# The S5 group's state carried over every fourth token instead of every second

## The chip, the cores and the metric

The kernel runs on one core of a Trainium2 chip. The metric is the device time of one execution in microseconds (us); before the change it was 1253.27 us (median of three runs, 1252.76 to 1253.33).

Names used below: TensorE (PE in the profile; its weight loads are PEld), VectorE (DVE), ScalarE (ACT), GpSimd (POOL) and SyncE (SP, which issues nearly all DMAs). SBUF is the on-chip memory, PSUM the accumulators that TensorE writes.

## The reference

One layer of a streaming encoder over 16 learned meta tokens and 256 tokens (T = 272 in all), D_MODEL = 2048, everything in float32: RMSNorm, one projection, two groups of heads side by side (HGRN2, a gated recurrence, and S5, a diagonal complex state-space model), one output projection, and a gated MLP with a short convolution. The part that the change rewrites is the S5 group: 64 channel groups of 16 inputs and 64 complex states each.

```python
def s5_mixer(u, lam_re, lam_im, log_step, b_re, b_im, c_re, c_im, d_skip, w_glu, b_glu, gain):
    ...
    ab_re = mag * jnp.cos(a_im * dt)
    ab_im = mag * jnp.sin(a_im * dt)
    ...
    bb_re = z_re[..., None] * br - z_im[..., None] * bi
    bb_im = z_re[..., None] * bi + z_im[..., None] * br
    bu_re = jnp.einsum('blgh,gph->lbgp', ug, bb_re)
    bu_im = jnp.einsum('blgh,gph->lbgp', ug, bb_im)
    ...
    _, _, st_re, st_im = lax.associative_scan(_complex_scan_combine, (a_seq_re, a_seq_im, bu_re, bu_im), axis=0)
    y = (jnp.einsum('lbgp,ghp->blgh', st_re, c_re.astype(f32))
         - jnp.einsum('lbgp,ghp->blgh', st_im, c_im.astype(f32)))
    y = y.reshape(b_sz, seq_len, D_S5) + d_skip.astype(f32) * uf
    y = jax.nn.gelu(y)
    y = y * jax.nn.sigmoid(y @ w_glu.astype(f32) + b_glu.astype(f32))
    return rmsnorm(y, gain)
```

## The kernel before

**The large products.** The projection `w_in` is worked off in chunks of 256 output columns, in the order `u0 h0 u1 h1 u2 h2 u3 h3 g0 g1 g2 g3` (u: S5 inputs, h: the HGRN2 heads' parts, g: their output gates). Each weight of 1 MB comes by one DMA on SP's queue (`raw`), ScalarE casts it to a rounded half `whi` (L160) and VectorE takes the rest, `wlo = raw - whi` (helper `tt`, L82); three buffers of each. `mm3` then multiplies three ways: high by high, high by low, low by high (L184 to L186, output `acc`, 272 columns). One `wlo` tile serves 24 of these matmuls. The MLP's gate and up products (`ga`, `ua`) and the down product (`d`) follow much later and are not touched.

**The S5 group** is worked in eight blocks j of 128 channels (8 channel groups, four pairs q of two groups). The 272 tokens are split into even and odd ones (TH = 136 of each), and the state is carried over every second token only. For a block:

- `s5_b(j)` prepares its tables: POOL multiplies B by the step (`bt1`, `bt2`, `br`), ScalarE copies `cp` from `cpc` (the output matrices, as they are and multiplied by the step) and lays out `eb`, TensorE transposes it (`btp`), and makes `ktp`, the direct product of C and B, from which ScalarE makes the short-range kernel `k0`.
- `s5_u`, `s5_split` copy the block's inputs into `ysb` and scatter them by four DMAs into `R`.
- `s5_tile(j)`: TensorE projects (`bu`, two rows of the array at a time, 64 rows by 128 columns). For each pair, `s5_scan` builds a table of rotations `W` of 136 columns from the 17 columns of `ew` by three doublings on ScalarE and VectorE, with the powers `pw[6]`, `pw[7]`, `pw[8]` (17, 34 and 68 steps), rotates `bu` (`P<-W,bu`), POOL adds the two halves (`m`), VectorE scans real and imaginary part (two scans of 136) and rotates back (`P<-W,m`, `xo`). TensorE then adds the short-range kernel (`yps<-ysb,k`, one matmul of 136 columns) and the states through `cp` (`yps<-xo,cp`), for even and odd tokens.
- Behind that stand GELU, the GLU product on the 258 columns from token T0 = 14 on, and the norm.

**The set-up** in front of it: POOL builds the powers `pw` of the rotation one from the other (`cpow`, per level two products `pt`, their sum `pw` and a negation) and, interleaved, the table `ew` of 16 columns by four doublings through `scb`; VectorE copies the 17th column (`ew<-pw`, L472) and makes `cpc`.

**The order.** The Tile framework schedules all instructions against a model of time and gives each engine one list, which it works off strictly in order; an instruction that waits holds back all behind it on its engine. Priorities (`pri`) tilt that order; the three-way products are given a lower priority than the rest and fill what is left.

Two places set how the S5 group meets the other work:

```python
        with pri(wpri[0]):
            pe.matmul(accs[m], lh, xh[:, n0:n1], start=first, stop=False)
```

```python
    for o in ORDER.split():
        {"u": do_u, "h": do_h, "g": do_g}[o[0]](int(o[1]))
```

The head work that shows up in the lists beside it is HGRN2's: `q`, `PP`, `SP`, `qh`, `kt`, `lps`, `dps`, `vtp`, `S`.

## Time and profile before

| | before |
|---|---|
| median of three runs | 1253.27 us |
| the profiled execution: its own time | 1252.36 us |
| its span | 1250.6 us |
| mean granted TensorE clock | 0.994 |
| TensorE busy | 1226.9 us |
| VectorE busy | 873.7 us |
| ScalarE busy | 601.2 us |
| POOL busy | 117.0 us |
| bytes read from HBM | 206.12 MB |

The profile is of one execution. A row of a view names the line of the kernel, the engine, the operation, the tile that is written and what is read, and shapes as partitions x elements. Lines of helpers stand for all that use them (L82 is every `tensor_tensor`, L91 every `scalar_tensor_tensor`, L79 every activation), so there the tile names tell the work. An idle time in front of an instruction is put down to the semaphore that came last. Matmul ends are modelled: what a matmul costs in the stream is read from the starts. A float32 matmul leaves two records.

### The profile page before, as it was taken

To read this page: it belongs to the slowest core of one execution; us is meant where nothing else is said; L and a number is where in the kernel's file an instruction comes from. 1 tells how busy PE (TensorE), PEld (TensorE's weight loads), DVE (VectorE), ACT (ScalarE), POOL (GpSimd) and SP (SyncE) were. 2 spreads that over 40 slices of the span, in tenths; PEclk is the share of its full clock that TensorE was granted. 3 is DMA by queue.
4 is the path that set the end of the run, shared out by engine and by line. 5 is a ranking of instruction groups with operands and counts; after the bars stand their busy time and mean duration, and the time that the engine had idled before them with its cause. 6 is when DMAs were issued, how large, how long until landed. Compare 5 with 4: busy or idle time off the path is not lost.

```text
span 1250.6 us, 22795 instructions
## 1 busy us (share of the span) xinstructions
PE 1226.9 (98%) x9299; PEld 1151.9 (92%) x9299; DVE 873.7 (70%) x1516; ACT 601.2 (48%) x1042; POOL 117.0 (9%) x165
## 2 busy tenths in 40 slices
PE   7989999999999999999999999999999999999997
PEld 6979898989989999999999999999999988888886
DVE  8989999999748867765665656656656645554554
ACT  5646767574545446343433433433434434444454
POOL 5483132221000000000000000000000000000000
PEclk9989999999999999999999999999999999999999
DMA  8533344243444565565556555555555545555552
GB/s 256 147 122 113 105 144 136 86 134 127 144 135 136 169 201 172 167 203 179 192 172 199 171 196 173 193 178 187 184 181 191 210 166 198 202 188 187 197 205 98
DMA packets 176298, 210.82 MB, mean 169 GB/s; under 512 B 14773, under 2 KB 168880, under 8 KB 170416
## 3 DMA queue, kind: packets, MB, share of 16 engines
q1 hardware_dynamic: 175871, 209.26, 51.1%
q8 instruction: 73, 1.20, 0.4%
q14 instruction: 34, 0.27, 0.1%
q0 software_dynamic: 320, 0.09, 0.0%
HBM read 206.12 MB, written 2.10 MB: 166 GB/s over the span
## 4 chain that ended last, share of the span: by engine, by line
PE 92%; DVE 3%; POOL 2%; issue 1%; DMA 1%; ACT 0%; SPq 0%; DVEq 0%; ACTq 0%; POOLq 0%
PE acc L186 9%; PE acc L184 8%; PE acc L185 8%; PE ua L185 7%; PE ua L184 7%; PE ga L184 7%; PE ua L186 7%; PE ga L186 7%; PE ga L185 7%; PE d L970 6%; PE d L969 6%; PE d L968 6%; PE lps L713 1%; PE bu L600 1%; DVE xn L91 1%
## 5 line engine op out<-in xcount | busy, mean ns | idle before, releaser
L82 DVE TENSOR_TENSOR wlo<-raw,whi 128x1024 fp32r<-128x1024 f32 (+1 forms) x376 | 461.4, 1227 | 320.8 <-ACT whi L160 271.2
L160 ACT CAST whi<-raw 128x1024 fp32r<-128x1024 f32 (+1 forms) x382 | 397.8, 1042 | 519.9 <-PE ga L185 158.3
L184 PE MATMUL ga<-fh,whi 128*128 128x258 f32 x704 | 199.0, 283 | 0.5 <-DVE a L82 0.5
L186 PE MATMUL ga<-fh,wlo 128*128 128x258 f32 x704 | 198.5, 282 | 0.0
L185 PE MATMUL ua<-fl,whi 128*128 128x256 f32 x704 | 198.4, 282 | 0.0
L185 PE MATMUL ga<-fl,whi 128*128 128x258 f32 x704 | 198.1, 281 | 0.0
L186 PE MATMUL ua<-fh,wlo 128*128 128x256 f32 x704 | 197.9, 281 | 0.0
L184 PE MATMUL ua<-fh,whi 128*128 128x256 f32 x704 | 197.9, 281 | 0.0
L186 PE MATMUL acc<-xh,wlo 128*128 128x272 f32 (+1 forms) x640 | 186.7, 294 | 5.0 <-DVE wlo L82 5.0
L185 PE MATMUL acc<-xl,whi 128*128 128x272 f32 (+1 forms) x640 | 186.1, 292 | 3.9 <-DVE xl L82 3.9
L184 PE MATMUL acc<-xh,whi 128*128 128x272 f32 (+1 forms) x640 | 186.4, 294 | 0.4 <-ACT PP L79 0.4
L184 PEld LDWEIGHTS ga<-fh,whi 128*128 128x128 f32 x704 | 133.0, 189 | 0.7 <-DVE a L82 0.7
L185 PEld LDWEIGHTS ga<-fl,whi 128*128 128x128 f32 x704 | 133.5, 190 | 0.0
L184 PEld LDWEIGHTS ua<-fh,whi 128*128 128x128 f32 x704 | 133.1, 189 | 0.0
L186 PEld LDWEIGHTS ua<-fh,wlo 128*128 128x128 f32 x704 | 132.9, 189 | 0.0
L185 PEld LDWEIGHTS ua<-fl,whi 128*128 128x128 f32 x704 | 132.8, 189 | 0.0
L186 PEld LDWEIGHTS ga<-fh,wlo 128*128 128x128 f32 x704 | 132.6, 189 | 0.0
L186 PEld LDWEIGHTS acc<-xh,wlo 128*128 128x128 f32 x640 | 121.4, 190 | 9.4 <-DVE wlo L82 5.6
L185 PEld LDWEIGHTS acc<-xl,whi 128*128 128x128 f32 x640 | 121.6, 190 | 7.5 <-DVE xl L82 4.8
L968 PE MATMUL d<-whi,ah 128*128 128x512 f32 x328 | 127.7, 389 | 0.0
L969 PE MATMUL d<-whi,al 128*128 128x512 f32 x328 | 127.6, 389 | 0.0
L184 PEld LDWEIGHTS acc<-xh,whi 128*128 128x128 f32 x640 | 121.1, 190 | 4.1 <-issue 2.0
(381 smaller groups left out, 1868.1 us busy)
## 6 DMA issues: line engine op xcount, KB each, us to landing
raw<-in_w_ffn_gate SPq DMA_DIRECT2D x44, 1024.0 KB, 5.1
raw<-in_w_ffn_up SPq DMA_DIRECT2D x44, 1024.0 KB, 5.1
raw<-in_w_ffn_down SPq DMA_DIRECT2D x44, 1024.0 KB, 4.8
raw<-in_w_in SPq DMA_DIRECT2D x39, 1024.0 KB, 5.2
raw<-in_w_out SPq DMA_DIRECT2D x16, 1024.0 KB, 5.8
raw<-in_w_glu SPq DMA_DIRECT2D x4, 1024.0 KB, 5.2
x<-in_x SPq DMA_DIRECT2D x4, 512.0 KB, 5.7
out<-ob SPq DMA_DIRECT2D x8, 256.0 KB, 2.7
```

What stands on the lines that cost most here:

```text
L82: eng.tensor_tensor(out=dst, in0=a, in1=b, op=op)
L91: dve.scalar_tensor_tensor(out=dst, in0=a, scalar=s, in1=b, op0=op0, op1=op1, **kw)
L160: act.copy(out=hi[:, c], in_=raw[:, hf, c])
L184: pe.matmul(accs[m], lh, xh[:, n0:n1], start=first, stop=False)
L185: pe.matmul(accs[m], lh, xl[:, n0:n1], start=False, stop=False)
L186: pe.matmul(accs[m], ll, xh[:, n0:n1], start=False, stop=end)
L600: return pe.matmul(bus[i][:, ri], bt[h, 2 * ri + q0 // 2], R[h, q0 // 2], start=True, stop=True)
L713: pe.matmul(ps[:, i], lhs[i], qf[:, 64 * i:64 * (i + 1)], start=True, stop=True)
L968: pe.matmul(dps[t][n], ah[:, tk], hi, start=False, stop=False, skip_group_check=True)
L969: pe.matmul(dps[t][n], al[:, tk], hi, start=False, stop=False, skip_group_check=True)
L970: pe.matmul(dps[t][n], ah[:, tk], lo, start=False, stop=end, skip_group_check=True)
```

## The change

The state is carried over every fourth token. TH becomes 68, tokens are held in four phases, and the tables and instructions are regrouped:

- Four channel pairs share an instruction: `s5_rot` builds one `W` of four times 68 columns by two doublings (`pw[7]`, `pw[8]`: 17 and 34 steps), the products `P`, `m` and `xo` are 4 x 68 wide, and one scan of 544 elements takes the place of eight of 136 per block. Its factor is a table `r4t` that is zero at each pair's first column. `m` is added on VectorE, no longer on POOL. Buffers of `bu`, `W`, `P`, `m`, `xo`, `bt` and the kernels go to one each.
- `bu` is projected by matmuls of 64 rows by 64 columns and 68 tokens (128 of them for 64 of twice the width and twice the columns).
- The short range reaches over three tokens: three kernels `kz`, from `ktp` (48 columns for 32) by a masked product `kw` on VectorE and three transposes `kwp`, streaming 204, 136 and 68 columns. `yps<-xo` is 32 matmuls of 68 or 67 columns per block for 16 of 136 or 135.
- `cpc` and `cp` have four kinds rather than two; POOL computes the two new ones from the old by `a2`, the step of two tokens, in eight instructions. B is multiplied by one and by two steps on POOL.
- `R` is scattered by eight DMAs per block instead of four; the powers are 1 to 64, 68 and 136 (not 34), so the 17th column of `ew` takes `pw[6]`, and the doublings of `ew` start one level later.
- The S5 columns behind are 260 (four phases of 65) for 258; `w_out` reads 258 of them, from QS = 2 on.

Lines move by four: L82 is now L86, L88 L92, L91 L95, L160 L164, L184 to L186 L188 to L190.

```diff
+NPH = 4
-TH = T // 2
-K0 = T0 // 2
+TH = T // NPH
+K0 = T0 // NPH
...
-    NPW = [1, 2, 4, 8, 16, 32, 34, 68, 136]
+    NPW = [1, 2, 4, 8, 16, 32, 64, 68, 136]
...
-    for d_, a_, b_ in ((1, 0, 0), (2, 1, 1), (3, 2, 2), (4, 3, 3), (5, 4, 4), (6, 5, 1), (7, 6, 6), (8, 7, 7)):
+    for d_, a_, b_ in ((1, 0, 0), (2, 1, 1), (3, 2, 2), (4, 3, 3), (5, 4, 4), (6, 5, 5), (7, 6, 2), (8, 7, 7)):
         cpow(d_, a_, b_)
+    a2 = s5p.tile([128, 2, NP], F32, name="a2")
+    tt(a2, pw[:, 1, 1:3], r2.unsqueeze(1).to_broadcast([128, 2, NP]), MUL, pool)
...
-    for lv, n in ((1, 1), (2, 2), (3, 4), (4, 8)):
+    for lv, n in ((2, 1), (3, 2), (4, 4), (5, 8)):
...
-        dve.tensor_copy(out=ew[:, :, k, 16:17], in_=pw[:, 5, k].unsqueeze(2))
+        dve.tensor_copy(out=ew[:, :, k, 16:17], in_=pw[:, 6, k].unsqueeze(2))
...
+    for hb in range(2):
+        cv = cpc[:, 16 * hb:16 * hb + 16]
+        c4 = [z.rearrange("p j h -> p (j h)").rearrange("p (j k r h) -> p j k r h", k=2, r=2, h=S5H)
+              for z in (cth[0], cth[1])]
+        for z, w in zip(c4, (a2[:, 0], a2[:, 1])):
+            tt(z.rearrange("p j k r h -> p j (k r h)"), cv[:, :, 0:2].rearrange("p j k r h -> p j (k r h)"),
+               w[:, 16 * hb:16 * hb + 16].unsqueeze(2).to_broadcast([128, 16, 4 * S5H]), MUL, pool)
+        tt(cv[:, :, 2:4, 0], c4[0][:, :, :, 0], c4[1][:, :, :, 1], ADD, pool)
+        tt(cv[:, :, 2:4, 1], c4[0][:, :, :, 1], c4[1][:, :, :, 0], SUB, pool)
...
+        for n, ar, ai in ((1, abr[:, js], xi[:, js]), (2, a2[:, 0, js], a2[:, 1, js])):
+            src, dst = bp[:, 4 - n:4], bp[:, 4 - 2 * n:4 - n]
...
+            for t, a in ((t1, ar), (t2, ai)):
+                tt(t[:, 0:n].rearrange("p s r j h -> p (s r) j h"), src.rearrange("p s r j h -> p (s r) j h"),
+                   a.unsqueeze(1).unsqueeze(3).to_broadcast([128, 2 * n, 4, S5H]), MUL, pool)
...
+        ktp = ptp.tile([128, 3, S5H], F32, tag="tp", name="ktp")
         for ri in range(2):
             for q in range(4):
+                pe.matmul(ktp[32 * q:32 * q + 32], cp[:, q, 0, ri].rearrange("p g h -> p (g h)"),
+                          bp[:, 1:4, ri, q], start=(ri == 0), stop=(ri == 1), skip_group_check=True)
...
+        tt(kw, ktp.unsqueeze(2).to_broadcast([128, 3, 8, S5H]),
+           misc[:, 26:34].unsqueeze(1).unsqueeze(3).to_broadcast([128, 3, 8, S5H]), MUL)
+        tp = ptp.tile([128, 3, 128], F32, tag="tp", name="kwp")
+        for k in range(3):
+            pe.transpose(tp[:, k], kw[:, k].rearrange("p g h -> p (g h)"), ident)
+        act.copy(out=kz, in_=tp)
...
+            for g in range(2):
+                c = 32 * q + 16 * g
+                sp.dma_start(out=R[h:h + 64, q % 2, g], in_=ysb[c:c + 16, j])
...
+        for lv, n in ((7, 17), (8, 34)):
+            c, sn = (pw[:, lv, i, js].unsqueeze(1).unsqueeze(3).to_broadcast([128, 2, 4, n]) for i in (1, 2))
+            tmp, tmq = (P[:, i].rearrange("p b (j n) -> p b j n", j=4) for i in range(2))
+            tt(tmp[:, :, :, 0:n], W[:, 0:2, :, 0:n], sn, MUL)
+            tt(tmq[:, :, :, 0:n], W[:, 1:3, :, 0:n], c, MUL)
+            tt(W[:, 1:3, :, n:2 * n], tmq[:, :, :, 0:n], tmp[:, :, :, 0:n], ADD)
+            fact(W[:, 0, :, n:2 * n], W[:, 2, :, n:2 * n], AF.Copy, scale=-1.0)
...
+                    for g in range(2):
+                        gr = slice(64 * g, 64 * g + 64)
+                        pe.matmul(bu[gr, i, (2 * ri + p) * TH:(2 * ri + p + 1) * TH], bt[h, 2 * ri + p, gr], R[h, p, g],
+                                  start=True, stop=True)
...
+        dve.tensor_tensor_scan(out=mf, data0=r4t[0].rearrange("p r j k -> p (r j k)"),
+                               data1=mf, initial=0.0, op0=MUL, op1=ADD)
+        tt(P, rot(None), m.unsqueeze(1).to_broadcast([128, 2, 2, 4 * TH]), MUL)
...
+        for k in range(3):
+            pe.matmul(yps[:, k:3], kz[:, 2 - k], ysb[:, j, 0:3 - k], start=(k == 0), stop=False, skip_group_check=True)
+        for p in (3, 0, 1, 2):
+            o, c, n0 = (0, 0, 0) if p == 3 else (1, p + 1, 1)
+            for ri in range(2):
+                for q in range(4):
+                    pe.matmul(yps[32 * q:32 * q + 32, p, n0:TH], cp[:, q, c, ri].rearrange("p g h -> p (g h)"),
+                              xo[:, ri, q, 0:TH - n0], start=False, stop=(ri == 1), skip_group_check=True)
```

The lists of the engines change at these places, all in the first block of the S5 group. A row names line, operation, the tile written and those read, and the engines whose semaphores it waits for.

First VectorE, where the copies of `pw` into `ew` stand. Before:

```order
L82 TENSOR_TENSOR PP<-PP 128x272 [waits DVE_49]
L472 COPY ew<-pw 128x32 [waits Pool_49]
L472 COPY ew<-pw 128x32
L472 COPY ew<-pw 128x32 [waits Pool_49]
L82 TENSOR_TENSOR wlo<-raw,whi 128x1024 [waits PE_49,Activation_49]
L91 SCALAR_TENSOR_TENSOR cpc<-sca 128x32x16 [waits DVE_49]
```

and with the change (`P<-W,pw` is the table's first doubling):

```order
L86 TENSOR_TENSOR PP<-PP 128x272 [waits DVE_49]
L86 TENSOR_TENSOR wlo<-raw,whi 128x1024 [waits PE_49,Activation_49]
L95 SCALAR_TENSOR_TENSOR cpc<-sca 128x32x16 [waits DVE_49]
L480 COPY ew<-pw 128x32 [waits Pool_49]
L480 COPY ew<-pw 128x32
L86 TENSOR_TENSOR qh<-q,PP 128x256 [waits DVE_49]
L86 TENSOR_TENSOR SP<-SP,PP 128x136x2
L86 TENSOR_TENSOR S<-dps,ident 128x512 [waits PE_49]
L480 COPY ew<-pw 128x32 [waits Pool_49]
L86 TENSOR_TENSOR wlo<-raw,whi 128x1024 [waits DMAHW7_49,PE_49,Activation_49]
```

The `wlo` that stood behind all three copies stands ahead of them; the next `wlo` stands behind the last copy.

Second POOL, at the end of its set-up. Before:

```order
L88 TENSOR_SCALAR pw<-pw 128x32 [waits Pool_49]
L82 TENSOR_TENSOR pt_485<-pw 128x64
L82 TENSOR_TENSOR pt_486<-pw 128x64 [waits Pool_49]
L82 TENSOR_TENSOR pw<-pt_485,pt_486 128x64 [waits Pool_49]
L88 TENSOR_SCALAR pw<-pw 128x32 [waits Pool_49]
L82 TENSOR_TENSOR pt_485<-pw 128x64
L82 TENSOR_TENSOR pt_486<-pw 128x64 [waits Pool_49]
L82 TENSOR_TENSOR pw<-pt_485,pt_486 128x64 [waits Pool_49]
L88 TENSOR_SCALAR pw<-pw 128x32 [waits Pool_49]
```

and with the change (`a_521` is `a2`; `scb` holds the products):

```order
L86 TENSOR_TENSOR pt_487<-pw 128x64
L86 TENSOR_TENSOR pt_488<-pw 128x64 [waits Pool_49]
L86 TENSOR_TENSOR scb<-cpc,a_521 128x1024 [waits DVE_49,Activation_49]
L86 TENSOR_TENSOR scb<-cpc,a_521 128x1024
L86 TENSOR_TENSOR pw<-pt_487,pt_488 128x64 [waits Pool_49]
L86 TENSOR_TENSOR cpc<-scb 128x16x2x16 [waits Pool_49]
L86 TENSOR_TENSOR cpc<-scb 128x16x2x16
L92 TENSOR_SCALAR pw<-pw 128x32 [waits Pool_49]
L86 TENSOR_TENSOR scb<-cpc,a_521 128x1024 [waits Pool_49]
```

Between the last two powers stand four instructions for the first half of the two new kinds of `cpc`; the second half follows the last `pw`, which is `pw[8]`. What VectorE has for it:

```order
L86 TENSOR_TENSOR P<-W,pw 128x8x34 [waits DVE_49,Pool_49]
L86 TENSOR_TENSOR wlo<-raw,whi 128x1024 [waits DMAHW0_49,PE_49,Activation_49]
L86 TENSOR_TENSOR qh<-q,PP 128x256 [waits DVE_49]
L86 TENSOR_TENSOR P<-W,pw 128x8x34 [waits Activation_49]
L86 TENSOR_TENSOR W<-P 128x8x34 [waits DVE_49]
L750 COPY_PREDICATED S<-masks,lps 128x128x2 [waits PE_49]
L86 TENSOR_TENSOR kt_619<-k,SP 128x32x8
L86 TENSOR_TENSOR SP<-SP,PP 128x34x8 [waits DVE_49]
L86 TENSOR_TENSOR wlo<-raw,whi 128x1024 [waits Activation_49]
L86 TENSOR_TENSOR P<-W,bu 128x4x136 [waits Activation_49]
```

The row with 34 columns waits for POOL, and the `wlo` rows stand behind it.

Third ScalarE and TensorE. ScalarE at the copies of `cp`, before:

```order
L540 COPY cp_588<-cpc 64x16x16 [waits DVE_49]
L540 COPY cp_588<-cpc 64x16x16
L540 COPY cp_589<-cpc 64x16x16 x2
L160 CAST whi<-raw 128x1024 [waits PE_49]
L79 ACTIVATE W<-W 128x17 [waits DVE_49] x2
```

and with the change:

```order
L559 COPY cp_599<-cpc 64x32x16 [waits Pool_49]
L559 COPY cp_599<-cpc 64x32x16
L559 COPY cp_600<-cpc 64x32x16 x2
L164 CAST whi<-raw 128x1024 [waits PE_49,Activation_49]
L83 ACTIVATE W<-W 128x4x34 [waits DVE_49]
L164 CAST whi<-raw 128x1024 [waits DMAHW1_49,PE_49,Activation_49]
L164 CAST whi<-raw 128x1024 [waits PE_49,Activation_49]
```

The copies waited for VectorE and now wait for POOL; the casts `whi` of the next weights stand behind them in both lists. TensorE, where the direct product `ktp` stands, before (behind the 379th `acc` matmul):

```order
L185 MATMUL acc<-xl,whi 128x272
L550 MATMUL ktp<-cp_588,eb 32x32 [waits PE_49,Activation_49]
L550 MATMUL ktp<-cp_588,eb 32x32
L713 MATMUL lps<-qh,k 128x64 [waits DVE_49]
L713 MATMUL lps<-qh,k 128x64 x3
L550 MATMUL ktp<-cp_588,eb 32x32 x6
L186 MATMUL acc<-xh,wlo 128x272
```

and with the change (behind the 421st `acc`):

```order
L188 MATMUL acc<-xh,whi 128x272
L575 MATMUL ktp<-bp,cp_599 32x48 [waits Activation_49,Pool_49]
L575 MATMUL ktp<-bp,cp_599 32x48 x3
L575 MATMUL ktp<-bp,cp_599 32x48 [waits DMAHW4_49,Pool_49]
L575 MATMUL ktp<-bp,cp_599 32x48 x3
L189 MATMUL acc<-xl,whi 128x272
```

In the new list `ktp` waits for ScalarE's copies and for POOL, and the matmuls of all other work stand behind it. The first `yps` on `xo` stands behind the 494th `acc` in the new list; in the old one behind the 592nd.

## What was predicted

> **What bounds the kernel now.** I read the page first, then the windows of core 0, then the waits of TensorE, the timeline of the one place where it waits long, and the chain of waits around it.
>
> ```profile
> PE 1226.9 (98%) x9299; PEld 1151.9 (92%) x9299; DVE 873.7 (70%) x1516; ACT 601.2 (48%) x1042; POOL 117.0 (9%) x165
> ...
> PE 92%; DVE 3%; POOL 2%; issue 1%; DMA 1%; ACT 0%; SPq 0%; DVEq 0%; ACTq 0%; POOLq 0%
> ...
> core 0: us, PE busy (x) PEld busy (x) DVE busy (x) ACT busy (x) POOL busy (x), PEclk, DMA share, GB/s
> 60.00:80.00 20.00, 15.70 (x124) 14.70 (x122) 18.47 (x33) 6.41 (x11) 20.00 (x30) 0.99 0.33 106
> 120.00:400.00 280.00, 280.00 (x2427) 254.55 (x2424) 245.63 (x513) 170.00 (x433) 48.33 (x55) 1.00 0.41 129
> ...
> 79.50:89.70 10.20, 8.73 (x49) 0.50 0.50 156
> ```
>
> TensorE is busy 98% of the span. From 120 to 400 us, where nearly all S5 work lies, it is busy 280.00 of 280.00 us. VectorE is at 245.63 of 280 there and ScalarE at 170, so what the change saves on those two saves nothing by itself there: nobody waits for them. What can be gained or lost is TensorE's own work, and the stretch between 60 and 120 us, where TensorE does wait (15.70 of 20 us) and POOL is busy 20.00 of 20.00. The last row shows a price that comes behind the wait: for 10.2 us the granted clock was 0.50.
>
> ```profile
> PE acc L186 <- DVE wlo L82: 4.6, 2, 3.6
> ...
> 24.00:28.00 4.00, 2.75 (x21) 1.00 0.33 113
> ...
> 77.17 1.46 POOL L82 TENSOR_TENSOR ew<-scb 128x512 f32<-128x512 f32 x1
> 78.94 0.86 DVE L472 COPY ew<-pw 128x32 f32<-128x32 f32 x3 [1.43 <-POOL pw L82]
> 79.70 1.21 DVE L82 TENSOR_TENSOR wlo<-raw,whi 128x1024 fp32r<-128x1024 f32 x1
> 80.97 0.60 PE L186 MATMUL acc<-xh,wlo 128*128 128x272 f32 x1 [3.61 <-DVE wlo L82]
> ```
>
> The long wait, 3.61 us, is laid to VectorE's `wlo`, but VectorE itself had stood 1.43 us before its copies of `pw` into `ew`, in front of that `wlo` in its queue, until POOL's power table was there. So POOL's set-up chain sets this place. With the half clock behind it (8.73 us of work in 10.2 us at 0.50, so some 4.4 us lost) it costs 8 us. That is all the change can win outside TensorE's own work.
>
> **The change, part by part.** *The start.* In the new order of VectorE the `wlo` stands ahead of the copies. VectorE can start it when its `PP` ends at 77.5, it takes 1.2 to 1.8 us beside POOL, and the first wait shrinks from 3.6 to about 1.7 us. But two things behind it are new. POOL now computes two more kinds of `cpc`, eight instructions, in front of the last power `pw[8]`; and ScalarE's `cp` copies, which waited for VectorE's `cpc`, now wait for POOL's, with the casts of the next weights queued behind them. VectorE's rotation (`P<-W,pw` of 34 columns) waits for `pw[8]` with two `wlo` behind it, and TensorE's `ktp` waits for the `cp` copies with all further matmuls behind it.
>
> ```profile
> 73.89 2.58 POOL L82 TENSOR_TENSOR scb<-ew,pw 128x512 f32<-128x512 f32 x2
> 82.15 0.77 POOL L82 TENSOR_TENSOR pt<-pw 128x64 f32<-128x64 f32 x2
> 106.44 0.76 POOL L82 TENSOR_TENSOR m<-P 128x272 f32<-128x272 f32 x1 [1.29 <-DVE P L82]
> 114.43 2.37 POOL L82 TENSOR_TENSOR m<-P 128x272 f32<-128x272 f32 x1 [7.22 <-DVE P L82]
> ...
> L540 ACT COPY cp<-cpc x16: 389/403/407, 82.3 to 264.4; 64x256 f32<-64x256 f32 x16
> ```
>
> POOL's chain up to the last `pt` ended at 82.92 before. It gains one power and `a2` (five small operations of 0.2 to 0.3 us) and larger products for `bt`, and some of the second token block's products move behind it: I put its end at 82.5 to 84.8, and take 83.7. Then come two products of 1024 elements, a `pw`, and two writes of 512, before `pw[8]` and `cp` go on. One of 512 took 1.29 in the first row and 1.46 at 77.17; one of 1024 does not occur, and lies between 1.8 (272 elements took 0.76, so 512 to 1024 adds some 0.65 to 1.1) and 2.9 (twice 1.46). Alone the block takes 6.1 to 9.0 us; beside VectorE the same `m<-P` took 0.76 once and 2.37 once, so it may stretch to 13.6. I take 9.6: `pw[8]` at 93.5, bounds 88.8 and 97.5. The two `cp` copies add 0.6 each (0.40 for half the elements): `ktp` can go at 94.7.
>
> ```profile
> 0.00:80.90 80.90, 49.66 (x366) 0.99 0.59 176
> 0.00:94.94 94.94, 60.22 (x420) 0.95 0.58 173
> 0.00:110.38 110.38, 71.18 (x493) 0.95 0.54 160
> ```
>
> These windows of TensorE's `acc` alone count its matmuls (busy time, then their number): 366 by the long wait, 420 by 94.94, 493 by 110.38. In the new order `ktp` stands behind the 421st. TensorE, resumed at 78.9 and at full clock, gets there after 54 of them and two groups of eight `lps`, 70 matmuls at the 0.115 us of the row from 120 to 400 (2427 in 280 us), so at about 87, and waits some 7.5 us, longer than the wait that halved the clock before. Up to there the change has lost nothing (94.7 against 94.95), but it has not used its head start, and it goes on at half clock.
>
> The next stop is `yps` on the first `xo`, which stood behind the 592nd `acc` and stands behind the 494th now. For that `xo` VectorE has 29 instructions from the one that waits for `pw[8]`.
>
> ```profile
> L82 DVE TENSOR_TENSOR wlo<-raw,whi 128x1024 fp32r<-128x1024 f32 x74 | 91.6, 1238 | 25.0 <-ACT whi L160 24.8
> L586 DVE TENSOR_TENSOR_SCAN m<-r,m 128x136 f32<-128x136 f32 x64 | 25.1, 427 | 2.9 <-POOL m L82 2.9
> L82 DVE TENSOR_TENSOR P<-W,bu 128x544 f32<-128x544 f32 x32 | 22.8, 711 | 1.2 <-ACT W L79 1.2
> ```
>
> Four `wlo` (4.95), fourteen of 256 to 272 elements at 0.43 (6.0), three masked copies at 0.55 (1.65), two products of 544 at 0.71, `m` and `xo` at about 0.71 each, the product of 1088 as two of 544 (1.42), `kw` and `km` 0.75, and the scan of 544: between 0.43 and four times that, I take 1.3. That is 18.9, all told, less 0.09 overlap each: 16.3 us. [...] So `xo` comes at 93.5 + 16.3 + 5 = 114.8, bounds 105.1 and 125.3. TensorE did the 494th `acc` at 110.39, and had by then done some 2.5 us of S5 and head work that the new order puts later (five `bu`, six `vtp`, a `ktp`, less `kwp` and `kz`). Net: 114.8 + 2.5 - 110.4 = **+7 us**, bounds -3 and +17. If the last wait before `xo` (about 3 us) halves the clock once more, 4.4 come on top.
>
> [...]
>
> *TensorE's own work.*
>
> ```profile
> 102.50 0.66 PE bu L600 x6
> 108.17 0.43 PE bu L600 x2
> 208.26 0.60 PE yps L614 x16
> 208.86 0.46 PE yps L619 x16
> 239.49 0.23 PE yps L610 x2
> 91.89 0.44 PE btp L545 x4
> 267.33 0.28 PE ktp L550 x15
> ...
> L614 PEld LDWEIGHTS yps<-xo,cp x128: 106/109/113, 126.5 to 314.0; 128*32 128x32 f32 x128
> ```
>
> A `bu` group of two records takes 0.43 us and one of six 0.66, so 0.31 for the interruption and 0.058 a record. Each j has two of each: 2.18 us, 17.4 in all. After, a j has 32 records of half the columns, in two groups by the order. No row shows four 64x64 quarters at once; `yps` runs four column tiles at once, 16 records of 136 columns in 0.46. Four at once gives 0.46 + 0.62 a j, two at once 0.93 + 0.62: a saving of 5.0 to 8.8 us; I take 7, nearer `yps`. The three short kernels stream 408 columns where one streamed 136: 0.69 for 0.23, +3.7. Three more transposes of 0.11 (`btp`: four in 0.44): +2.6, and up to 2.5 more where they interrupt by themselves. `ktp` is half as wide again: +0.4, at most 1. GLU has 260 columns for 258 on 192 matmuls: +0.2. `yps` has twice the records, half as long: 0 if the columns count. Each loads weights for 110 ns, against 58 ns of columns; if that shows, it is 16 loads a tile, 1.76 for 0.93, +6.6 us. Against it, 15 `ktp`, whose weights have 32 columns as well, finish in 0.28. I take 0. Sum: -7 + 3.7 + 2.6 + 0.4 + 0.2 = **0**, ends -2 and +12.
>
> [...]
>
> *Nothing* I give to VectorE's and ScalarE's shorter lists (cover: TensorE's full 280 us), to `m` moved from POOL (same), and to the scatter of R, where eight DMAs a block stand on SP's queue for four.
>
> ```profile
> L566 SPq DMA_DIRECT2D R<-ysb x32: 537/597/1018, 40.6 to 260.4; - x32
> ```
>
> Four more issues of 0.6 us delay the weights behind them on SP by 2.4 us a block; three buffers of weights cover it. Without the cover it would be those 2.4 us for eight blocks, 19 us, but no row has TensorE waiting for a weight's DMA behind 60 us.
>
> Sum: 1252.4 (the profiled execution) + 7 + 0 = 1259.4. The median of the runs stands 0.9 above that execution: **1260**.
>
> **The rivals.** *Faster, by a chain that POOL does not hold.* The point of decision is the first `xo` at 107.9, where the start comes out even. If POOL's 1024 elements take 1.8 us and VectorE is not disturbed, `pw[8]` comes at 88.8, `xo` at 105.1, and with 2 us less on TensorE the time is 1253.3 - 3 - 2 = 1248. For it: the first wait is shorter, and between 24 and 28 us TensorE stood 1.25 us without losing the clock (1.00 in the row of that window). Against: POOL was full from 60 to 80 and gets more.
>
> *The stall only moves.* `pw[8]` at 91, `xo` at 107 to 109: 1252 to 1255.
>
> *Small matmuls cost by their weights.* With +6.6 for `yps` and `bu` at two at once: 1260 + 9 = 1269. For it the 110 ns, against it `ktp`.
>
> *Two clock drops.* 1260 + 4.4 = 1265; it belongs to the forecast's upper half.
>
> **How the numbers follow.** The forecast with its clock drop (1256 to 1268) 0.46, the faster rival 0.22, the moved stall 0.19, the dear weights or a later `xo` 0.13. About 0.2%, 2.5 us, is what a measurement of this kernel can tell from no change. So faster 0.22, same 0.19, slower 0.59. The range leaves out the tenth at each end: 1247 to 1273.
>
> **What would show it.** Right: a wait of TensorE at `ktp` of 4 us or more, put down to ScalarE's `cp`, with POOL's `cpc` behind it; a clock of 0.50 after it; a second wait at the first `yps` on `xo`, at 112 us or later; from 140 us on no waits. `bu` at 1.1 us a j and `kz` at 0.7 show TensorE's terms. Wrong: POOL's 1024 elements under 1.8 us; `ktp` met without a wait; `yps` over 1.5 us a j.

## The result and the profile after

The changed kernel takes **1267.96 us** (median of 4 runs, 1267.46 to 1268.88) against 1253.28: a ratio of **1.0123** [1.0111, 1.0136], slower by 14.7 us. The forecast was 1260, slower by 7. The sign was right; the size is twice the forecast, and half of the loss lies where none was forecast. The profiled execution of the changed kernel took 1267.46 us.

The first fence is the page of the changed kernel: the busy time of each engine, and the shares of the chain that ended last.

```profile
PE 1224.8 (97%) x9739; PEld 1155.7 (91%) x9739; DVE 850.0 (67%) x1365; ACT 565.6 (45%) x826; POOL 114.1 (9%) x156
...
PE 84%; DVE 7%; POOL 4%; issue 2%; DMA 2%; ACT 1%; SPq 1%; DVEq 0%; POOLq 0%; ACTq 0%
```

Every engine has less work than before (TensorE 1224.8 us for 1226.9, VectorE 850 for 874, ScalarE 566 for 601), and the kernel is slower. TensorE's share of the chain fell from 92% to 84%; VectorE and POOL, 5% together before, now hold 11%. So the loss is waiting, and it lies early: the first gate matmul of the part behind S5 (`ga`) starts at 508.28 us for 493.46 before, 14.8 us later, which is nearly the whole difference of the two executions (spans of 1265.7 and 1250.6 us).

The windows of the changed kernel place it (stretch; its length, then busy time of TensorE, its weight loads, VectorE, ScalarE and POOL; then the granted clock).

```profile
62.00:120.00 58.00, 44.34 (x354) 42.73 (x356) 56.47 (x80) 19.69 (x32) 46.11 (x54) 0.85 0.36 112
120.00:200.00 80.00, 72.72 (x926) 67.86 (x922) 65.52 (x122) 41.27 (x80) 21.57 (x25) 1.00 0.33 98
200.00:420.00 220.00, 219.31 (x2066) 202.15 (x2064) 157.62 (x279) 106.23 (x191) 14.89 (x27) 1.00 0.43 134
```

TensorE's idle time, length less busy, was 5.27, 0.00 and 0.40 us in these three before. It is now **13.66, 7.28 and 0.69**: 8.4 us more up to 120 us, and 7.6 behind it, where I had forecast none. The waits of TensorE from 60 to 420 us name who ended them (line, waited for; us in total, times, longest).

```profile
PE lps L747 <- DVE S L750: 8.5, 2, 4.6
PE dps L719 <- DVE q L95: 4.4, 2, 3.4
PE lps L747 <- DVE S L86: 2.8, 2, 1.8
PE btp L569 <- ACT bq L565: 2.2, 1, 2.2
PE mps L783 <- DVE sm L90: 1.6, 1, 1.6
...
```

The two long ones are TensorE's `lps` on VectorE's masked copy into `S`. The `wlo` wait of before is gone, and neither my `ktp` nor my first `xo` is among the waits. Three timelines of the changed kernel show what happened there: POOL, VectorE, TensorE (start, us, instruction; in brackets the idle time before it).

```profile
87.40 4.80 POOL L86 TENSOR_TENSOR scb<-cpc,a 128x1024 f32<-128x1024 f32 x2
...
92.49 2.88 POOL L86 TENSOR_TENSOR cpc<-scb 128x512 f32<-128x512 f32 x2
95.35 0.26 POOL L92 TENSOR_SCALAR pw<-pw 128x32 f32<-128x32 f32 x1
95.58 4.14 POOL L86 TENSOR_TENSOR scb<-cpc,a 128x1024 f32<-128x1024 f32 x2
99.79 3.55 POOL L86 TENSOR_TENSOR cpc<-scb 128x512 f32<-128x512 f32 x2
```

```profile
88.44 3.91 DVE L86 TENSOR_TENSOR P<-W,pw 128x136 f32<-128x136 f32 x2
...
92.73 1.51 DVE L86 TENSOR_TENSOR SP<-SP,PP 128x272 f32<-128x272 f32 x1
94.16 0.72 DVE L750 COPY_PREDICATED S<-masks,lps 128x256 f32<-128x256 int32 x1
...
95.82 2.14 DVE L86 TENSOR_TENSOR P<-W,pw 128x272 f32<-128x272 f32 x1
97.88 2.92 DVE L86 TENSOR_TENSOR wlo<-raw,whi 128x1024 fp32r<-128x1024 f32 x1
100.72 1.49 DVE L86 TENSOR_TENSOR qh<-q,PP 128x256 f32<-128x256 f32 x1
102.13 1.51 DVE L86 TENSOR_TENSOR P<-W,pw 128x272 f32<-128x272 f32 x1
```

```profile
95.03 1.90 PE L747 MATMUL lps<-qh,kt 128*128 128x64 f32 x8 [4.56 <-DVE S L750]
...
104.89 1.33 PE L747 MATMUL lps<-qh,kt 128*128 128x64 f32 x5 [3.91 <-DVE S L750]
```

POOL's block runs from 87.40 to 95.35 and from 95.58 to 103.3, 3.7 us later than I took it to start, and its 1024 elements take 2.4 and 2.1 us each, in my bounds of 1.8 to 2.9. But VectorE is not waiting at its end; it is busy, with instructions that take several times as long as elsewhere. Two products of 136 elements take 3.91 us together; at 138.10, for a later block, they take 0.51.

Behind 120 us the engine to look at is ScalarE. Its timeline of the changed kernel, and POOL's of the same time:

```profile
156.80 1.18 ACT L565 COPY bq<-bp 128x256 f32<-128x256 f32 x2 [5.80 <-POOL bp L86]
157.88 1.04 ACT L164 CAST whi<-raw 128x1024 fp32r<-128x1024 f32 x1
```

```profile
149.87 0.40 POOL L86 TENSOR_TENSOR bt<-bp,abr 128x128 f32<-128x128 f32 x1 [18.60 <-DMA bp<-in_s_b_im]
...
150.71 1.95 POOL L86 TENSOR_TENSOR bp<-bt,bt 128x64 f32<-128x64 f32 x2
152.73 3.10 POOL L86 TENSOR_TENSOR bt<-bp,a 128x256 f32<-128x256 f32 x2
155.91 0.86 POOL L86 TENSOR_TENSOR bp<-bt,bt 128x128 f32<-128x128 f32 x2
```

ScalarE stands 5.80 us in front of its copies `bq`, until POOL has made the eight products of B's block, and behind `bq` in its queue stands the next cast of weights `whi`, which VectorE's `wlo` needs. (POOL had itself stood until B's DMA had landed; `bp` has one buffer.) No wait of TensorE's `acc` for a `wlo` is among the waits. TensorE waits for `bq` itself (`btp`, 2.2 us), and for what stands in VectorE's queue behind a `wlo` that is waiting. The block before shows such a case: `bq` waited 4.07 us for POOL there, until 131.30. Then VectorE's `wlo` waited for the cast behind `bq`; from there VectorE worked nearly without a pause down to `sm` (140.35), and TensorE's `mps` waited for that.

```profile
133.49 1.23 DVE L86 TENSOR_TENSOR wlo<-raw,whi 128x1024 fp32r<-128x1024 f32 x1 [4.21 <-ACT whi L164]
...
140.61 0.39 PE L783 MATMUL mps<-qm,km 128*16 128x258 f32 x1 [1.65 <-DVE sm L90]
```

### The profile page after: what moved, and what is told of

It reads as the page before. It is cut to its first block, busy times and chain, and to the rows that moved or that the text cites. A ratio compares the mean times of both kernels' runs of the same rounds, so it can differ in the third digit from the quotient of the medians.

```text
span 1265.7 us, 23347 instructions
## 1 busy us (share of the span) xinstructions
PE 1224.8 (97%) x9739; PEld 1155.7 (91%) x9739; DVE 850.0 (67%) x1365; ACT 565.6 (45%) x826; POOL 114.1 (9%) x156
## 4 chain that ended last, share of the span: by engine, by line
PE 84%; DVE 7%; POOL 4%; issue 2%; DMA 2%; ACT 1%; SPq 1%; DVEq 0%; POOLq 0%; ACTq 0%
PE acc L188 7%; PE acc L190 7%; PE acc L189 7%; PE ua L189 7%; PE ua L188 7%; PE ga L188 7%; PE ua L190 7%; PE ga L190 7%; PE ga L189 7%; PE d L1004 6%; PE d L1002 6%; PE d L1003 6%; DVE wlo L86 1%; PE lps L747 1%; DVE P L86 1%
## 5 line engine op out<-in xcount | busy, mean ns | idle before, releaser
L86 DVE TENSOR_TENSOR wlo<-raw,whi 128x1024 fp32r<-128x1024 f32 (+1 forms) x376 | 463.7, 1234 | 344.0 <-ACT whi L164 294.2
L164 ACT CAST whi<-raw 128x1024 fp32r<-128x1024 f32 (+1 forms) x382 | 397.8, 1043 | 544.5 <-PE ga L189 158.3
L188 PE MATMUL ga<-fh,whi 128*128 128x258 f32 x704 | 199.0, 283 | 0.5 <-DVE a L86 0.5
L190 PE MATMUL ga<-fh,wlo 128*128 128x258 f32 x704 | 198.5, 282 | 0.0
L190 PE MATMUL ua<-fh,wlo 128*128 128x256 f32 x704 | 197.9, 281 | 0.0
L188 PE MATMUL ua<-fh,whi 128*128 128x256 f32 x704 | 197.9, 281 | 0.0
L190 PE MATMUL acc<-xh,wlo 128*128 128x272 f32 (+1 forms) x640 | 187.5, 295 | 0.0
L188 PE MATMUL acc<-xh,whi 128*128 128x272 f32 (+1 forms) x640 | 187.1, 295 | 0.4 <-ACT PP L83 0.4
L188 PEld LDWEIGHTS ga<-fh,whi 128*128 128x128 f32 x704 | 133.0, 189 | 0.7 <-DVE a L86 0.7
L188 PEld LDWEIGHTS ua<-fh,whi 128*128 128x128 f32 x704 | 133.1, 189 | 0.0
L190 PEld LDWEIGHTS ua<-fh,wlo 128*128 128x128 f32 x704 | 132.9, 189 | 0.0
L190 PEld LDWEIGHTS ga<-fh,wlo 128*128 128x128 f32 x704 | 132.6, 188 | 0.0
L188 PEld LDWEIGHTS acc<-xh,whi 128*128 128x128 f32 x640 | 122.5, 192 | 2.9 <-issue 1.7
L190 PEld LDWEIGHTS acc<-xh,wlo 128*128 128x128 f32 x640 | 122.9, 193 | 2.1 <-issue 1.3
```

Of the source, the lines that this page charges most:

```text
L86: eng.tensor_tensor(out=dst, in0=a, in1=b, op=op)
L164: act.copy(out=hi[:, c], in_=raw[:, hf, c])
L190: pe.matmul(accs[m], ll, xh[:, n0:n1], start=False, stop=end)
```

## The experiments

There were four theories. **A**: POOL's block of eight instructions on `cpc` in the set-up is the whole loss. **B1**: the late waits come from tiles with a single buffer (`bp`, `bt`, `kz`, and `kw` in `bq`'s). **D**: VectorE's set-up of `cpc` is too long for the new order. **P**: POOL's element-wise products themselves, since VectorE's instructions stretch beside them and ScalarE waits behind them. (In the expectations, B is a loss spread over the new lists, and O one that comes from their order; e11's P names a memory path, which no run shows.) The table gives medians, the ratio to the kernel before, run beside each, with its 95% interval, and TensorE's idle time in the three windows (62 to 120, 120 to 200, 200 to 420 us) of the profiled execution.

| run | us | ratio | TensorE idle |
|---|---|---|---|
| before | 1253.28 | | 5.27 / 0.00 / 0.40 |
| after | 1267.96 | 1.0123 [1.0111, 1.0136] | 13.66 / 7.28 / 0.69 |
| e1 after without POOL's block | 1264.04 | 1.0084 [1.0057, 1.0111] | 8.47 / 9.15 / 1.81 |
| e2 after, the block's work by block j, POOL | 1271.15 | 1.0143 [1.0123, 1.0163] | 8.90 / 8.19 / 5.05 |
| e3 the same, VectorE | 1259.89 | 1.0066 [1.0043, 1.0088] | 8.94 / 2.23 / 4.78 |
| e4 before with the block | 1259.64 | 1.0058 [1.0043, 1.0073] | 8.59 / 0.14 / 0.18 |
| e5 after, all of `cpc` by block, VectorE | 1259.43 | 1.0051 [1.0034, 1.0068] | 9.06 / 3.36 / 0.36 |
| e6 e5 with two buffers | 1255.86 | 1.0027 [1.0016, 1.0039] | 5.31 / 2.61 / 0.15 |
| e9 before, all of `cpc` by block, VectorE | 1252.58 | 0.9999 [0.9990, 1.0008] | 5.27 / 0.00 / 0.20 |
| e10 e6, one scratch tile shared with `m` | 1253.63 | 1.0009 [0.9999, 1.0019] | 4.80 / 3.17 / 2.14 |
| e11 e6, B's products on VectorE | 1245.34 | 0.9938 [0.9925, 0.9952] | 5.50 / 0.22 / 0.15 |
| e13 e10, B's products on VectorE | 1245.52 | 0.9940 [0.9927, 0.9952] | 3.04 / 0.00 / 1.62 |
| e14 before, B's products and `m` on VectorE | 1253.24 | 1.0002 [0.9994, 1.0011] | 4.27 / 0.00 / 0.82 |
| e15 after, B's products on VectorE | 1258.82 | 1.0043 [1.0030, 1.0057] | 10.97 / 0.64 / 0.71 |
| e12 e15, and the block on VectorE | 1248.27 | 0.9970 [0.9958, 0.9981] | 4.35 / 2.23 / 1.79 |
| e16 e11 with idle products on POOL | 1248.64 | 0.9966 [0.9954, 0.9978] | 4.84 / 0.52 / 0.15 |
| e17 e11 again, beside e16 | 1246.11 | 0.9943 [0.9931, 0.9956] | 3.54 / 0.27 / 0.31 |

**The block alone (e1, e2, e3, e4).** e1 puts a ScalarE copy in place of the block, so the two new kinds are not computed there; e2 and e3 make them in each of the eight blocks j of channels, on POOL and on VectorE; e4 gives the block to the kernel before, into a tile that nobody reads.

```diff
-    for hb in range(2):
-        ...                                   # the block's eight POOL instructions
+    act.copy(out=cpc[:, :, 2:4]..., in_=cpc[:, :, 0:2]...)          # e1
+        cv = cpc[:, js]                                             # e2, e3: in s5_b(j)
+        for z, w in zip(cts, (a2[:, 0, js], a2[:, 1, js])):
+            tt(z..., cv[:, :, 0:2]..., w..., MUL, pool)             # e3: dve
+        tt(cv[:, :, 2:4, 0], ..., ADD, pool)
+        tt(cv[:, :, 2:4, 1], ..., SUB, pool)
+        tt(cw[:, :, :, 0], c4[0]..., c4[1]..., ADD, pool)           # e4: before, unread
```

> The changed kernel without the eight POOL instructions that make the two new kinds of cpc; one ScalarE copy of the old kinds stands in their place, so kinds 2 and 3 hold wrong values. Theory A (POOL's block holds VectorE and with it TensorE): the waits of 4.6 and 3.9 us between 90 and 105 us and the half clock behind them (4.5 us) go, so 11 to 13 us less, 1255 to 1258 us. Theory B (the loss is spread over the new lists: the early start, the wait on q, the waits behind 120 us; the block is one of many): 3 to 6 us less, 1262 to 1265 us.

> The same work as the changed kernel, but the two new kinds of cpc are made block by block on POOL (256 and 128 elements an instruction, 1/8 of the work in front of the first block). Theory A: nearly all of e1's gain, 1256 to 1260 us. Theory B: 1262 to 1266 us. A third way: the small products of the later blocks disturb VectorE as often as the large ones did, and the time stays at 1266 to 1270 us.

> As e2, with these products on VectorE. Theory A: like e2 or 1 to 2 us better, since VectorE's own 256 elements take 0.43 us and POOL's twice that and block it: 1254 to 1259 us. Theory B: 1262 to 1266 us.

> The kernel before with the changed kernel's a2 and the eight POOL instructions added behind cpc (same shapes, results unused). Theory A: TensorE stalls between 85 and 110 us here too, 5 to 11 us more, 1258 to 1264 us. Theory B: the old lists carry it, 1252 to 1256 us.

e4 takes 7.0 us more than the kernel before beside it (1252.60), and it shows up to 120 us: 3.3 us more idle time and a lower clock there (0.85 for 0.91). So the block alone costs about as much as my start term said, though not by the waits that I had put there. But taking it out of the changed kernel gives back only 3.9 us in the median (e1). Its five runs lie between 1258.36 and 1267.59, so that gain is known to 3 or 4 us only, and the profiled execution is the slowest of them: in it the early waits shrink by 5.2 us, and the late ones grow from 8.0 to 11.0. A is not the whole of it. On POOL by block (e2) nothing is gained; on VectorE (e3) 8.1 us are. That was the first hint that the engine counts more than the place.

**Set-up length and buffers (e5, e6, e8, e9, e10).**

```diff
-    for kind, (wr, wi) in enumerate(((zr, zi), (zar, zai))):        # e5: set-up of cpc, out
-        ...
+        cv = s5w.tile([128, 4, NPH, 2, S5H], F32, tag="cpc", bufs=1)  # e5: by block, on VectorE
+        ...
-        bp = s5w.tile(..., tag="bp", bufs=1)                        # e6; bt and kz likewise
+        bp = s5w.tile(..., tag="bp", bufs=2)
-        kw = s5w.tile(..., tag="bq", bufs=1)
+        kw = s5w.tile(..., tag="kw", bufs=1)
-        cts = [s5w.tile(..., tag=f"cc{i}", bufs=1) for i in range(2)]
+        cts = [s5w.tile(..., tag=('m', 'cc1')[i], bufs=1) for i in range(2)]   # e10
```

> The changed kernel with all four kinds of cpc made block by block on VectorE (16 small instructions, some 3 us a block, in a buffer of one block), so the set-up loses twelve VectorE instructions of 512 elements (about 9 us) and POOL's eight. Theory D (before 120 us TensorE waits for VectorE, which is full there and slowed by POOL; whatever leaves VectorE's list before the first block shortens the waits): the waits at 67, 83 and 90 to 105 us (13.7 us) shrink to some 4, the later ones (8.4 us) stay, 1252 to 1258 us. Theory O (the list's order makes the waits; the work is taken up by others): 1260 us or more.

> e5, and with the SBUF that it frees two buffers for bp, bt and kz and a buffer of its own for kw, which shared one with bq. Theory B1 (the waits behind 120 us come from the single buffers: the next block's btp waits for bq, which waits for kw's transposes and for bp): they go, 4 to 8 us less than e5. Theory B2 (they come from VectorE's and POOL's list, whose instructions are longer than the scheduler holds them to be): the same as e5 within 2 us.

> e6 a second time, for one more profile: the waits are the same to 0.3 us each, and what differs between the two profiles is the stretch at half clock (0 to 6 us).

> The kernel before with its two kinds of cpc made block by block on VectorE as in e5 and nothing else. Theory D: VectorE's set-up loses some 9 us, so the waits of 1.0, 0.6 and 3.6 us between 66 and 81 us shrink or go and with them the half clock: 1244 to 1250 us, and then e6's gain was the set-up's and the four-token state is still slower. Theory O: the old list has nothing to gain there, 1251 to 1256 us.

> e6, with one of the two work buffers of the cpc products put into the buffer of m, so that the next block's products can't be run ahead of this block's scan. Theory D (VectorE's list in front of 90 us is what counts): the waits at 67 and 87 us (2.9 and 1.9) shrink to 2 in all, 1250 to 1254 us. Theory O: other waits of the same size, 1254 to 1259 us.

e5 is no better than e3, and in the kernel before the edit that takes the set-up of `cpc` apart changes nothing (e9): D falls. Second buffers give 3.6 us (e6 against e5), less than the 4 to 8 of B1, so B1 holds a part, and 2.6 us of waits from 120 to 200 us stay. e10 takes 2.2 us less than e6, which is in D's range for it; but with B's products off POOL the same edit is worth nothing (e13 against e11 below), so it doesn't carry D. e8 is one more execution of e6's kernel: 1255.9 us. One more run, e7, put the chunk `h0` ahead of `u0` in the changed kernel and took 1262.73 us (1.0081); that kernel doesn't compute this layer, and nothing here rests on it.

**The products off POOL (e11, e13, e14, e15, e12).** The edit is the last argument of six calls; e15 makes it at B's products in `s5_b`, e12 also at the block in the set-up.

```diff
-                   a..., MUL, pool)
+                   a..., MUL)
-            tt(f(dst, 0), f(t1, 0), f(t2, 1), SUB, pool)
-            tt(f(dst, 1), f(t1, 1), f(t2, 0), ADD, pool)
+            tt(f(dst, 0), f(t1, 0), f(t2, 1), SUB)
+            tt(f(dst, 1), f(t1, 1), f(t2, 0), ADD)
```

> e6, with the products that prepare B (bp, eight instructions a block) on VectorE too, so that POOL touches no block behind the set-up. Theory P (POOL's share of the memory path stretches VectorE's instructions): VectorE's rows between 60 and 90 us get shorter, waits 2 to 4 us less than e6, 1251 to 1255 us. Theory V (VectorE has no room for 2 us more a block): waits grow, 1256 to 1262 us.

> The changed kernel with only the eight instructions a block that prepare B on VectorE; POOL keeps the eight for cpc in the set-up. Theory P: the waits behind 120 us go (8 us), those between 90 and 105 us stay: 1256 to 1262 us.

> The changed kernel with the eight instructions of the two new kinds of cpc and the eight a block that prepare B on VectorE instead of POOL; nothing else is moved, buffers as in the changed kernel. Theory P (what costs is POOL working beside VectorE): nearly all of the loss goes, 1248 to 1255 us, and the waits behind 120 us are under 2 us. Theory B1 (the single buffers): the waits behind 120 us stay at 4 to 8 us, 1256 to 1262 us.

> e11 with e10's edit: the best of both, if the two gains add: 1243 to 1246 us; if the waits at 67 and 70 us (5.0) are the set-up's on VectorE, as theory D has it, no better than e11, 1245 to 1248 us.

> Control: the kernel before with its products for B and its m on VectorE instead of POOL. Theory P: it had no wait behind 90 us for POOL to cause, and VectorE gets some 25 us more work that TensorE's full stretch hides; the waits of 66 to 81 us may shrink by the products that POOL loses there: 1248 to 1254 us.

From the changed kernel itself, with every buffer as it was: B's products on VectorE take 9.1 us off (e15), the block on VectorE another 10.6 (e12), together **19.7**, and the kernel is then faster than before. The windows of e15 show that its gain is mostly the late one: idle time from 120 to 200 us is 0.64 for 7.28, and from 62 to 120 still 10.97.

```profile
62.00:120.00 58.00, 47.03 (x366) 45.40 (x364) 56.54 (x91) 20.58 (x32) 39.12 (x39) 0.85 0.35 113
120.00:200.00 80.00, 79.36 (x986) 73.08 (x985) 70.70 (x155) 47.02 (x91) 1.11 (x2) 1.00 0.38 113
```

The groups of ScalarE from 105 to 420 us point to the mechanism (busy time, mean ns; idle time before them and who ended it): the changed kernel, then e15.

```profile
L565 ACT COPY bq<-bp 128x256 f32<-128x256 f32 x14 | 8.5, 652 | 22.9 <-POOL bp L86 20.8 <-DMA R<-ysb 2.1
```

```profile
L565 ACT COPY bq<-bp 128x256 f32<-128x256 f32 x14 | 8.6, 661 | 7.5 <-DVE bp L86 7.5
```

ScalarE stood 20.8 us in front of `bq` for POOL's products, and stands 7.5 for VectorE's. VectorE is not done much sooner: for the block shown above POOL took 6.9 us from the first product to the last, VectorE in e15, between its other work, 6.4 (153.95 to 160.34). What also differs is the order, which the scheduler makes anew for each kernel: the third block's `bq` stands behind 36 casts of weights in e15's list, and behind 31 in the changed kernel's. So e15 shows that B's products on POOL, with the lists that come with them, cost 9.1 us; how much of that is the engine and how much the order is not shown. (O was not run for itself.)

In e12's timeline of VectorE the instructions of the early stretch have their own length again, and the products that had taken POOL 4.80 us take VectorE 2.35.

```profile
82.79 0.50 DVE L86 TENSOR_TENSOR P<-W,pw 128x136 f32<-128x136 f32 x2
83.21 1.21 DVE L86 TENSOR_TENSOR wlo<-raw,whi 128x1024 fp32r<-128x1024 f32 x1
...
88.75 0.41 DVE L86 TENSOR_TENSOR qh<-q,PP 128x256 f32<-128x256 f32 x1
89.08 0.43 DVE L86 TENSOR_TENSOR SP<-SP,PP 128x272 f32<-128x272 f32 x1
89.43 0.78 DVE L86 TENSOR_TENSOR P<-W,pw 128x272 f32<-128x272 f32 x2
...
91.27 2.35 DVE L86 TENSOR_TENSOR scb<-cpc,a 128x1024 f32<-128x1024 f32 x2
```

Against these, VectorE's instructions between 88.4 and 103.6 us of the changed kernel took 3.91 + 2.14 + 1.51 for 0.50 + 0.78 (`P`), 2.92 for 1.21 (`wlo`), 1.49 for 0.41 (`qh`) and 1.51 for 0.43 (`SP`): **10.2 us** more in a stretch of 15. e14 shows that products on POOL do not cost by themselves: in the kernel before, B's products (and `m`) moved to VectorE change nothing (1.0002). e11 is the fastest kernel of the study, 0.9938 of the kernel before; e13 is no better.

**Held up, or waited for? (e16, e17).** P has two halves. e16 keeps POOL at B's products without anyone waiting for them: they go into a tile that nobody reads, and the order of the instructions on TensorE, VectorE and ScalarE is that of e11 (and of e17, its control on the same chip).

```diff
+        if j > 1:
+            for n, a in ((1, abr[:, js]), (2, a2[:, 0, js])):
+                for i in range(2):
+                    tt(dum[:, 0:2 * n], bp[:, 3] if n == 1 else dum, a..., MUL, pool)
+                for i in range(2):
+                    tt(dum[:, 0:n], dum[:, n:2 * n], dum[:, 0:n], SUB, pool)
```

> The fastest kernel so far (four kinds by block, two buffers, B's products on VectorE) with POOL given the eight products of B a second time from the third block on, into a tile of 256 elements that nobody reads. The order of the instructions on TensorE, VectorE and ScalarE is the same to the row, and no engine waits for POOL. Theory P1 (a POOL product holds VectorE's two-operand instructions up while it runs): B's eight blocks on POOL cost 9.1 us in the changed kernel, so six should cost 3 to 7 here: 1248 to 1252, with 1.5 us or more of TensorE's waits from 120 to 420 us where this kernel had 0.37, and a longer mean of VectorE's P<-W,pw. Theory P2 (B's products were late because POOL takes longer over them, and VectorE's loss is slight): nobody waits for these, so 1245.3 within 1 us and no waits.

> The same kernel without the idle products, a second time, on the chip of the run beside it: 1245.3 within 1 us by both theories; the difference between the two is what is asked.

e16 takes 2.5 us more than e17 (0.9966 and 0.9943, their intervals just touch): in the range of P1 (1248 to 1252), but less than the 3 to 7 us that P1 asked for. The windows from 120 to 200 us, first of e16, then of e17:

```profile
120.00:200.00 80.00, 79.48 (x893) 72.88 (x892) 79.83 (x190) 44.12 (x83) 34.06 (x26) 1.00 0.43 131
```

```profile
120.00:200.00 80.00, 79.73 (x888) 73.44 (x887) 76.56 (x185) 44.11 (x85) 1.10 (x2) 1.00 0.43 133
```

VectorE is busy 3.3 us longer from 120 to 200 us beside POOL's 34 us of work, and TensorE's late waits do not come back (0.67 us from 120 to 420 us for 0.58); 1.3 us of the 2.5 lie between 62 and 120 us. So B's short products hold VectorE up a little, and it is likely, though argued and not shown, that what made them dear in the changed kernel is ScalarE's wait for them. One limit: e16 stands on the kernel with second buffers, not on the changed kernel.

For the block with its 1024 elements e4 tells the two halves apart. Nobody reads there what the block makes, and between 81 and 120 us VectorE waits for POOL nowhere; still its instructions stretch while the block runs (87 to 95 and 95 to 100 us), and TensorE's `lps` waits 2.7 us for `S` behind them:

```profile
89.91 2.14 DVE L82 TENSOR_TENSOR SP<-SP,PP 128x272 f32<-128x272 f32 x1
...
95.39 2.93 DVE L82 TENSOR_TENSOR wlo<-raw,whi 128x1024 fp32r<-128x1024 f32 x1
```

Elsewhere in that trace they take 0.43 and 1.21. So the block holds VectorE up.

## Why the prediction was right in its sign and wrong in its size

The sum as measured, at the first `ga` matmul: idle time +8.4 (62 to 120 us) and +7.6 (behind), half clock about +2, the first 62 us +1.6 (14 `acc` matmuls fewer done by then, at a clock of 0.92 for 1.00, which also varies between executions of one kernel, as the last section shows), TensorE's own S5 work -3.5: 16.1 against the 14.8 seen there.

**The step that failed** is "*Nothing* I give to VectorE's and ScalarE's shorter lists (cover: TensorE's full 280 us)", and with it "from 140 us on no waits". Measured: 7.6 us of waits behind 120 us, 5.5 of them behind 140, nearly the whole miss of 8 us. A shorter list was taken for an earlier engine. I had counted the larger products of `bt` only in POOL's chain of the set-up and didn't ask, for the other blocks, who stands behind them. ScalarE's `bq` does, with the casts behind it: VectorE stood 17.6 us before its `wlo` for `whi` from 60 to 300 us, and 2.2 in the kernel before. TensorE was busy 280.00 of 280 in the kernel before because nothing came late; that said nothing of how much later things could come. e15 takes these waits away by moving B's products alone (and with the order that follows from it).

**The start, +7 (bounds -3 to +17).** Right in its stretch and its engine, too small: idle time and half clock together come to about +10.4. POOL's `pw[8]` came at 95.6 (I took 93.5), by two errors that nearly cancel. The block took 8.0 us for my 9.6, but it began at 87.40 for my 83.7, outside my bounds: I had taken the last `pt` but one for the last, and a power more, where both kernels make eight. The last `pt` of the kernel before ended at 85.59:

```profile
84.64 0.95 POOL L82 TENSOR_TENSOR pt<-pw 128x64 f32<-128x64 f32 x2
```

The wait for `wlo` did vanish, though one of 3.4 us for `q` came at 67.5 to 70.9: TensorE's 401st `acc` ran at 89.05 us for 90.87 before, and the 426th at 106.99 for 97.62. The mechanism was half right. The 5 us by which the sum lets POOL's work delay VectorE (0 to 11.5 in its bounds) were my estimate, and no run shows that term; 10.2 is what the long rows give. And TensorE did not stop at `ktp`, which it met without a wait (a sign of being wrong that I had named), nor at `xo`, which came at 118.4 for my 114.8; it stopped at `lps`, whose next group needs VectorE's `S`, queued among the stretched instructions. The two products of 136 elements, 3.91 us for the pair against 0.50 in e12, each ended 0.16 us behind one of POOL's two of 1024 (90.44 and 92.35 us, POOL's at 90.28 and 92.19). Why, the trace does not show.

**The clock.** Predicted 4.4 us more or none by whether a second drop comes. Behind 62 us there were two stretches at half clock in the changed kernel, one of 3.4 and one of 13.6 us:

```profile
71.20:74.60 3.40, 3.40 (x18) 3.40 (x17) 3.40 (x5) 0.25 (x1) 3.40 (x4) 0.50 0.88 299
95.10:108.70 13.60, 9.69 (x55) 9.00 (x56) 13.53 (x14) 4.04 (x8) 13.18 (x14) 0.50 0.08 11
```

TensorE's second long wait (3.9 us) lies inside the longer one. The `acc` matmuls start 0.23 us apart in them, and 0.13 at full clock, so I take half of the busy time of both, some 6.5 us, as their cost, for the 4.4 of before. So the second drop came, and added 2 us rather than 4.4, since the first cost only 1.7; why one lasted 3.4 us, one 10.2 and one 13.6 stays open.

**TensorE's own work, 0 (ends -2 and +12).** Measured -3.5 by busy time, in which the modelled ends of neighbours overlap. The groups of TensorE's S5 lines from 62 to 420 us, before and after (busy us, mean ns):

```profile
L600 PE MATMUL bu<-R,bt 64*128 64x136 f32 x128 | 18.9, 314 | 0.1
L614 PE MATMUL yps<-xo,cp 128*32 128x136 f32 x128 | 6.3, 286 | 0.0
L619 PE MATMUL yps<-xo,cp 128*32 128x135 f32 x128 | 5.7, 279 | 0.0
```

```profile
L653 PE MATMUL yps<-xo,cp 128*32 128x67 f32 (+1 forms) x512 | 10.6, 224 | 0.4 <-DVE xo L86 0.4
L626 PE MATMUL bu<-R,bt 64*64 64x68 f32 x256 | 9.8, 230 | 0.4 <-DMA R<-ysb 0.4
L648 PE MATMUL yps<-ysb,kz 128*128 128x204 f32 (+2 forms) x48 | 7.5, 292 | 0.0
```

`bu` saves 9.1 us, a little above the upper end of my 5.0 to 8.8. Quarters of 64 by 64 do run four at once: a group of 32 records took 0.70 us at 66.77, where four at once would give 0.77 and two at once 1.24 by my prices. `yps` with its 512 weight loads is busy 1.4 us less, not 6.6 more, so the rival of dear weights falls. The three short kernels came as forecast (7.5 us for 3.5); their transposes took 4.3 us where I had 2.6, inside what I had allowed, and `ktp` 1.3 less (3.7 for 5.0).

**The rivals.** The faster one needed VectorE undisturbed beside POOL. e12, where POOL has no such products, comes out at 1248.27, and the rival's figure was 1248; that is agreement by luck, since its sum was another. So is the 1269 of the dear weights, near the 1268 measured: the weights weren't dear. The moved stall fails: the stall grew.

## What to carry to other kernels

When a change makes an engine's list shorter, ask of each product that stays on POOL which in-order queue waits for it and what stands behind that waiter; "TensorE was full there" only says that nothing was late so far. Here POOL's products were paid twice beside a busy VectorE, in POOL's own time (4.80 us for the two of 1024 elements, 2.35 on VectorE) and in VectorE's stretch (10.2 us in 15): 72 instructions, moved to VectorE, were worth 19.7 us although VectorE was the busier engine, and in the kernel before a like move was worth nothing (1.0002). And a part that is taken out of a kernel with several late chains can give back less than it is worth once the others are gone (the block: 3.9 us in e1, where the runs scatter, and 10.6 in e12): the next chain is already there.

## What the runs showed of the hardware beyond that

In e16 POOL's products stretch beside VectorE, some for the length of several of its instructions. Nine of e16's twelve POOL products of 64 elements took 0.3 to 1.2 us, the other three 5.3 to 6.7. Two of the three:

```profile
158.48 11.30 POOL L86 TENSOR_TENSOR dum<-dum 128x64 f32<-128x64 f32 x2
```

VectorE ran on nearly without a pause (busy 79.83 of 80 us from 120 to 200 us), and its `wlo` kept their length (1.24 us in the mean from 60 to 300 us, 1.22 in e17). So there POOL's products took longer and VectorE's `wlo` did not, which may be one more reason why e16's products cost so little.

And the early clock is not set by the kernel alone: two profiled executions of one kernel (e6 and e8) had 0.97 and 0.92 over the first 62 us.

```profile
0.00:62.00 62.00, 54.48 (x383) 0.97 0.66 195
```

```profile
0.00:62.00 62.00, 53.09 (x377) 0.92 0.66 195
```
